# Outputs of six expert pairs of the last layer sent through DRAM rows by token, in place of one-hot products

## The chip, the core and the metric

The program runs on one core of a Trainium2 chip. Its five engines work side by side: TensorE (PE, matrix products), VectorE (DVE), ScalarE (ACT), GpSimd (POOL) and SyncE (SP), and all DMA traffic of the core goes over 16 DMA engines. The metric is the device time of one execution in microseconds (us), lower is better; several executions are timed and their median is given. A profiled execution leaves a trace with the start and the length of every instruction, and of every DMA packet.

## What is computed

A diffusion transformer of two layers, in float32: 256 tokens `x`, 256 context tokens `ctx`, width 1024, 16 experts of width 256. The second layer is the last one and does its expert part for the 256 tokens of `x` alone. Cut to what matters here:

```python
def moe_ffn(h, w_router, router_bias, w_gate, w_up, w_down):
    ...  # each token takes the two best experts of one group of four
    gates = jnp.sum(jax.nn.one_hot(expert_idx, N_EXPERTS, dtype=f32) * w[..., None], axis=1)
    out = jnp.zeros_like(t)
    for e in range(N_EXPERTS):
        hid = jax.nn.silu(t @ w_gate[e]) * (t @ w_up[e])
        out = out + gates[:, e:e + 1] * (hid @ w_down[e])
    return out.reshape(shape)

# in the layer:  x = x + g2 * moe_ffn(hx, ...);  after the last layer:  rms_norm(x, final_g)
```

## The kernel before

Each token has exactly two experts, so the kernel computes an expert for the tokens that chose it alone. In the last layer the function `expert_pairs` takes the experts two at a time, pairs 0 to 7, each expert with a list of 64 places, so that a pair fills 128 places. A ninth unit (number NP = 8) is a single expert that has more tokens than 64 places hold. Which token stands in which place is kept in one-hot matrices `route.sel[i]` (128 tokens of tile i by all places, T = 2 tiles).

The steps of pair p, in the code's names: `gather` brings the tokens of four experts into their places by one-hot products (L1134); `half(p, 0)` and `half(p, 1)` are the gate and the up products (L1169; L1156 for the single expert) into the one bank `gu`; `hidden` is SiLU on ACT (L1179) and a product on DVE (L1180), which frees `gu`; `turn` transposes the hidden layer (L1190) and the one-hot places (L185) on PE; `down` is the third product (L1217); `evacuate` multiplies by gate and modulation on DVE (L1202) and splits the result in two float32r parts, `yh` on ACT (L1204) and `yl` on DVE (L1205); `add` sums both parts into four accumulators by one-hot products (L1235). At the end `sum_` adds the accumulators to x, and the last norm and the stores follow.

The loop runs over p, and PE's order in a turn of it is half(p,0), turn(p-1), add(p-2), half(p,1), down(p-1), gather. DVE, ACT, POOL and SP each take their own instructions in order; a scheduler wrote that order when the program was built.

Weights are 1 MB each (six per pair), issued by SP into 13 slots in the order of their use: a load starts when a slot has been read for the last time. The three weights of the single expert are chosen at run time and are loaded by POOL with an indirect DMA (L353). POOL's DMAs run on queue q0, SP's on q1, ACT's on q10; the last norm's weights `fg` are loaded by ACT (L233).

Of the kernel before, what the change touches and what calls it, by code (L numbers as in the profile page):

```python
# [23 lines left out]
D = 1024  # L24
# [8 lines left out]
# columns of the packed constants  # L33
C_COS, C_SIN, C_MASK, C_IOTA, C_TRI, C_LT, C_GW, C_TOK, C_MH, C_EXP, C_ROW, C_SUM, C_END = (
    0, 128, 256, 512, 640, 768, 784, 788, 796, 804, 820, 821, 837)

# slots for raw weights: throughout, from the output projection on, from the experts on
RAW = dict(A=4, B=(4, 3), C=(2, 5))
# halves of units as float32r parts: projections, their outputs' projections, experts
WSP = dict(proj=4, out=(4, 4), moe=5)  # L40
# banks of PSUM in the phases of a layer
# [17 lines left out]
TICK = (("sums", 1), ("high", 5), ("transposes", 0), ("evacuate", 0), ("weights", 1), ("finish", 0), ("scores", 3),  # L59
        ("low", 5), ("maxima", 3), ("finish", 2), ("finish", 1), ("exps", 3), ("rest", -1), ("values", -1))  # L60
# halves of experts' weights that are ready ahead of their products
LEAD = 4
OVERFLOW = True
# products that keep the array's clock up before the experts
# [7 lines left out]
def shape_constants():  # L72
    """Constants that depend on shapes alone, packed [128, C_END]."""
# [21 lines left out]
    k[:, C_SUM:C_END] = i % 32 == np.arange(16)  # L95
# [3 lines left out]
class Ring:  # L99
    """Weights in the order of their use, loaded ahead into whatever slots are free."""  # L100
# [11 lines left out]
    def open(self, pool, tag, n, last, queue=None):  # L112
        """n slots, for units of layers up to last"""
        self.free.extend((pool, f"{tag}{i}" if n > 1 else tag, last) for i in range(n))
        self.load(queue)
# [52 lines left out]
class Model:  # L168
# [38 lines left out]
    def rstd(self, pool, ss, n, width, tag):  # L207
        """(ss / n + eps) ** -0.5 over [128, width]"""
# [12 lines left out]
    def split(self, raw, lo, hi, engine=None):  # L221
        """A half of a unit of raw weights as an exact sum of two float32r parts."""
# [7 lines left out]
    def bcast(self, pool, tag, src, n, name, bufs=1, queue=None):  # L230
        """n elements in DRAM over all partitions"""
# [6 lines left out]
    def run(self, over):  # L238
        tc, nc, a = self.tc, self.nc, self.a
        self.over = over  # L240
        with ExitStack() as ctx:
# [9 lines left out]
            self.yrows = self.dram.tile([NEXP * SLOTS * max(self.npass), D], F32, name="yrows")  # L251
            self.ada_in()
# [25 lines left out]
    def queue(self):  # L278
        """The weights in the order of their use."""
# [15 lines left out]
        def block(name, l, cb, n):  # L295
            for h in range(2):
# [3 lines left out]
                if name == "w_out" and h:  # L300
                    # rows of heads (kind, key head, query) to chunks of (kind, query)
# [6 lines left out]
        for l in range(2):  # L308
# [28 lines left out]
    def warm(self, n):  # L337
        """Products that nothing uses: the array's clock is to be up when the next ones come"""
# [87 lines left out]
    def ada_third(self, l, third):  # L426
        """2048 columns of the modulation: the four 512s land on partitions 32j (c) and 32j+1 (c_ctx)."""
# [42 lines left out]
        elif third == 1:  # L470
            # what the shift adds to the router's logits, over all partitions
# [25 lines left out]
    # steps and the loads of units in a third of the modulation  # L497
    STEPS = (9, 10, 9)

    def fill(self, n):  # L500
        """n steps of the modulation among other work"""
# [3 lines left out]
    # rows of the modulation in DRAM: (third, half)  # L505
# [8 lines left out]
    def layer(self, l):  # L514
# [28 lines left out]
        self.nt2 = 8  # L543
        with self.psums(PS_ATT):
            self.attention(l)
# [33 lines left out]

    def t2(self, name):  # L580
# [8 lines left out]
    def parameters(self, l):  # L589
        """The small parameters of a layer's attention"""  # L590
# [19 lines left out]
        def lam():  # L610
            """-(exp1 - exp2 + lam0)"""
# [6 lines left out]
    def tokens_in(self, l, tl):  # L618
        """Steps that bring tiles of a stream, normalized and modulated, to d on the partitions in Xh and Xl"""
# [22 lines left out]
        # the chunks of d in a bank  # L642
# [35 lines left out]
    def chunk(self, ps, tiles, kc, parts):  # L678
        """The products of tiles with a chunk of d of the first block of the projections"""
# [7 lines left out]
    def first_in(self):  # L687
        """The tokens of the first layer, half of d after the other, with the first block of its projections"""
# [99 lines left out]
            # the context's tokens have had their last use  # L788
# [3 lines left out]
    def parts(self, name, l, cb, fill=(0, 0)):  # L792
        """The halves of two units, split"""
# [9 lines left out]
    def units(self, name, l, cb, pairs, xh, xl, c0, parts):  # L803
        """The products of tiles of tokens with 512 columns of a weight, a group of tiles after another."""
# [15 lines left out]
    def rope(self, dst, src, nh, t, view=lambda z: z):  # L820
        """dst, src: [128, nh * 64]"""
# [17 lines left out]
    def head_norm(self, src, nh, g):  # L839
        """src: [128, nh * 64] in PSUM -> SBUF"""  # L840
# [33 lines left out]
    def project_in(self, l, first):  # L874
        nc, nq = self.nc, self.nq
        tile_ = lambda name, *shape, dt=F32: self.qkv.tile([128, *shape], dt, name=name)
        # by head and map
# [5 lines left out]
        for i, cb in enumerate(CBS):  # L883
# [3 lines left out]
            for t, ps in products:  # L887
# [46 lines left out]
    def attention(self, l):  # L934
        """All heads, as a pipeline of items: two maps of scores of a tile of queries each."""
# [28 lines left out]
    def out_proj(self, l, work, mods):  # L964
        """x += g1 (mix w_out), and the routing of the tiles as they get ready"""
# [20 lines left out]
    def experts(self, l, mo, lists):  # L986
        """One expert after another, the second half of its layers among the next one's first half"""
# [4 lines left out]
        # halves of weights in the order of their use, some of them ahead of it  # L992
# [28 lines left out]
        def tokens(n):  # L1021
            """What an expert gets, with d on the partitions"""
# [10 lines left out]
        def first(n, b, s):  # L1033
            """Half the products of the gate or of the up projection"""
# [15 lines left out]
        def turn(n):  # L1050
            # f = p * 2 + c
# [55 lines left out]
    def expert_pairs(self, l, mo, route):  # L1107
        """Two experts at a time on halves of the columns of the array; gathers and sums by one-hot products."""
# [804 lines left out]
```

## Time and profile before

| | us |
|---|---|
| median of 3 timed runs (lowest, highest) | 903.25 (901.96, 904.15) |
| span of the profiled execution, first to last instruction | 900.9 |
| PE busy in it | 799.3 (89%) |
| DVE busy | 584.3 |
| ACT busy | 453.6 |
| POOL busy | 211.5 |
| chain that ended last: share of PE | 70% |

The span is that of one profiled execution; the timed runs hold what lies around the span as well, 2.4 us here by the median. Busy shares are means over stages that are limited by different things, so the stage of the change is read by itself, in stretches of the span.

### The profile page before, as it was taken

The numbers are of one execution on the slowest core, as the hardware profiler recorded it, in microseconds if no ns is written. First come the engines' busy times: TensorE is split into PE (matmuls) and PEld (weight loads), VectorE is DVE, ScalarE is ACT, GpSimd is POOL, SyncE is SP. The second block draws the span as 40 slices with busy tenths as digits, with TensorE's granted clock in tenths as the row PEclk, the third lists the DMA queues.
The fourth block names the chain that finished last, engine by engine and source line by source line (L and its number), as shares of the span: only waits on it lengthen the run. The fifth ranks groups of instructions, "written<-read, shape, count | busy, mean of one in ns | idle before, by whom it ended". The sixth has DMA issues, their size and how long they took to land.

```text
span 900.9 us, 13085 instructions
## 1 busy us (share of the span) xinstructions
PE 799.3 (89%) x4807; PEld 584.2 (65%) x4807; DVE 584.3 (65%) x1192; ACT 453.6 (50%) x877; POOL 211.5 (23%) x244
## 2 busy tenths in 40 slices
PE   4899999989889977999999459999799869999992
PEld 1578877545546746999999348767566647666551
DVE  1577673897942698899999487677587563231224
ACT  2454432777652426888888456443387442121112
POOL 2010102473320133443432561000442000000100
PEclk9999999999998998999999769999999988999996
DMA  9952221666579537899993754287035965999921
GB/s 320 346 171 92 93 94 47 249 227 235 181 239 343 192 141 261 310 402 399 402 406 146 256 202 187 90 327 281 0 132 152 354 245 220 406 406 407 378 84 51
DMA packets 52537, 213.34 MB, mean 237 GB/s; under 512 B 9756, under 2 KB 9756, under 8 KB 34672
## 3 DMA queue, kind: packets, MB, share of 16 engines
q1 hardware_dynamic: 40832, 182.34, 54.4%
q0 software_dynamic: 6752, 19.08, 6.3%
q10 hardware_dynamic: 4880, 11.00, 3.2%
q8 instruction: 40, 0.66, 0.3%
q14 instruction: 33, 0.27, 0.1%
HBM read 204.99 MB, written 11.60 MB: 240 GB/s over the span
## 4 chain that ended last, share of the span: by engine, by line
PE 70%; DVE 14%; issue 4%; DMA 4%; ACT 4%; POOL 3%; ACTq 0%; SPq 0%; POOLq 0%; DVEq 0%
PE mm L199 8%; PE mm L197 8%; PE mm L198 8%; PE gu L1169 7%; PE tp L185 5%; PE gu L199 4%; PE w L1217 3%; PE gu L197 3%; PE gu L198 3%; PE ada L448 3%; DVE nm L1407 2%; PE w L1134 2%; PE sc L1393 2%; PE acc L1235 2%; PE y L197 2%
## 5 line engine op out<-in xcount | busy, mean ns | idle before, releaser
L227 DVE TENSOR_TENSOR wlo<-wraw,whi 128x1024 fp32r<-128x1024 f32 x136 | 186.5, 1391 | 51.9 <-ACT whi L226 51.1
L226 ACT CAST whi<-wraw 128x1024 fp32r<-128x1024 f32 x152 | 153.0, 1050 | 73.5 <-PE mm L199 39.1
L197 PE MATMUL mm<-whi,Xh 128*128 128x512 f32 x288 | 117.9, 409 | 5.1 <-ACT Xh L670 4.7
L198 PE MATMUL mm<-wlo,Xh 128*128 128x512 f32 x288 | 115.6, 401 | 0.4 <-DVE wlo L227 0.4
L199 PE MATMUL mm<-whi,Xl 128*128 128x512 f32 x288 | 115.3, 400 | 0.5 <-DVE Xl L674 0.5
L213 POOL TENSOR_TENSOR rstd<-ms,cst 128x1 f32<-128x1 f32 (+2 forms) x36 | 30.2, 838 | 315.0 <-DVE ms L211 306.1
L1420 ACT ACTIVATE e<-sc,nm 128x512 f32<-128x512 f32 (+1 forms) x96 | 58.3, 613 | 37.1 <-DVE nm L1413 19.2
L199 PE MATMUL gu<-whi,xl 128*128 128x256 f32 x256 | 73.9, 289 | 0.2 <-DVE xl L1030 0.2
L197 PE MATMUL gu<-whi,xh 128*128 128x256 f32 x256 | 73.7, 288 | 0.3 <-ACT xh L1029 0.3
L198 PE MATMUL gu<-wlo,xh 128*128 128x256 f32 x256 | 72.3, 282 | 0.0
L197 PEld LDWEIGHTS mm<-whi,Xh 128*128 128x128 f32 x288 | 54.9, 191 | 23.9 <-ACT Xh L670 6.2
L199 PEld LDWEIGHTS mm<-whi,Xl 128*128 128x128 f32 x288 | 54.9, 191 | 14.6 <-DVE Xl L674 1.5
L198 PEld LDWEIGHTS mm<-wlo,Xh 128*128 128x128 f32 x288 | 55.1, 191 | 13.1 <-DVE wlo L227 1.2
L1169 PE MATMUL gu<-wraw,xq 128*64 128x256 f32 x512 | 62.5, 388 | 0.0
L227 POOL TENSOR_TENSOR wlo<-wraw,whi 128x1024 fp32r<-128x1024 f32 x16 | 42.5, 2656 | 81.3 <-ACT whi L226 50.3
L199 PEld LDWEIGHTS gu<-whi,xl 128*128 128x128 f32 x256 | 48.9, 191 | 1.3 <-DVE xl L1030 0.6
L1169 PEld LDWEIGHTS gu<-wraw,xq 128*64 128x64 f32 x512 | 36.2, 138 | 20.8 <-issue 4.1
L197 PEld LDWEIGHTS gu<-whi,xh 128*128 128x128 f32 x256 | 49.1, 192 | 0.5 <-ACT xh L1029 0.5
L198 PEld LDWEIGHTS gu<-wlo,xh 128*128 128x128 f32 x256 | 49.0, 191 | 0.0
L185 PEld LDWEIGHTS tp<-ident,e 128*128 128x128 f32 x240 | 26.3, 143 | 34.7 <-issue 15.3
L1407 DVE TENSOR_REDUCE nm<-sc 128x1 f32<-128x512 f32 x64 | 41.6, 684 | 10.9 <-PE sc L1393 7.2
L1180 DVE TENSOR_TENSOR hid<-hid,gu 128x256 f32<-128x256 f32 (+1 forms) x9 | 3.8, 422 | 64.9 <-ACT hid L1179 64.9
(329 smaller groups left out, 1689.2 us busy)
## 6 DMA issues: line engine op xcount, KB each, us to landing
wraw<-in_w_ada SPq DMA_DIRECT2D x40, 1024.0 KB, 4.7
wraw<-in_w_gate SPq DMA_DIRECT2D x32, 1024.0 KB, 9.6
wraw<-in_w_up SPq DMA_DIRECT2D x32, 1024.0 KB, 9.9
wraw<-in_w_down SPq DMA_DIRECT2D x32, 1024.0 KB, 8.6
wraw<-in_w_in SPq DMA_DIRECT2D x16, 1024.0 KB, 6.9
wraw<-in_w_ada SPq DMA_DIRECT2D x16, 512.0 KB, 8.0
yrows<-y ACTq DMA_DIRECT2D x16, 512.0 KB, 7.4
wraw<-in_w_out SPq DMA_DIRECT2D x4, 1024.0 KB, 7.8
```

Of the source, the lines that this page charges most:

```text
L185: self.nc.tensor.transpose(out, in_, self.k["ident"][:n, :n])
L197: mm(out, lhsT=xh, rhs=wh, start=start, stop=False)
L198: mm(out, lhsT=xh, rhs=wl, start=False, stop=False)
L199: mm(out, lhsT=xl, rhs=wh, start=False, stop=stop)
L213: nc.gpsimd.tensor_tensor(r, ms, self.k["mhalf"][:, :width], OP.pow)
L226: nc.scalar.copy(h, raw[:, lo:hi])
L227: (engine or nc.vector).tensor_tensor(l, raw[:, lo:hi], h.bitcast(F32), OP.subtract)
L448: nc.tensor.matmul(ps[32 * j:32 * j + 32, :], lhsT=self.silu_c[:, kc, :], rhs=raw[:, 512 * j:512 * j + 512], start=kc == 0, stop=kc == NKC ...
L1169: nc.tensor.matmul(gu[PSLOTS * g:PSLOTS * g + PSLOTS, 256 * b:256 * b + 256], lhsT=xq[q][:, kc, c:c + PSLOTS], rhs=raw[:, kc * 256:kc * 25 ...
L1217: nc.tensor.matmul(y[hf][gs], lhsT=hT[:, c, 0:PSLOTS] if p == NP else hT[:, c, gs], rhs=raw[:, c * D + o * 512:c * D + o * 512 + 512], sta ...
L1407: V.reduce_max(self.nm[:, i:i + 1], self.ps[i], axis=AX.X)
L1420: nc.scalar.activation(self.e[i][:, :self.nkey], self.ps[i], AF.Exp, scale=0.125, bias=self.nm[:, i:i + 1], accum_out=self.z[i])
```

## The change

In the first six pairs (`SCATTER = 6`) the outputs are no longer split, turned and added by one-hot products. `evacuate` writes one float32 tile `yr`, and POOL scatters its 128 rows with an indirect DMA to a DRAM tensor `prow` of 512 rows: each token has two rows, one for each of its experts. Places without a token carry a row number outside the tensor and are not written. `rows_back` reads `prow` back into four tiles of 128 x 1024, and `add_back` adds them to x on DVE. Pairs 6 and 7 and the single expert keep the old way. `prow` is cleared in the last layer's attention by one 2 MB store. The row numbers come out of the product that gave the gates by place, which now multiplies the places with 48 columns (`picks`: two parts of the gate, and the row) in float32r, in place of 16 in float32.

```diff
+SCATTER = 6
+            self.prow = self.dram.tile([PROWS, D], F32, name="prow")
...
+    def clear_rows(self):
+        z = self.per.tile([128, 512], F32, tag="modrow", name="zeros")
+        self.nc.gpsimd.memset(z, 0.0)
+        rows = self.prow[:, :].rearrange("(p a) (b n) -> p (a b) n", a=4, n=512)
+        self.nc.sync.dma_start(rows, z.unsqueeze(1).broadcast_to([128, 8, 512]))
...
         def turn(p):
...
             nc.scalar.copy(hT[:, :, :n], w[:, 0:2 * P2].rearrange("p (c s) -> p c s", s=P2)[:, :, :n])
+            if p < SCATTER:
+                return
             w = self.bank("w")
...
         def evacuate(p, o, y, g):
+            if p < SCATTER:
+                nc.vector.scalar_tensor_tensor(st[p]["y"][0][:, o], y, gates[:, p:p + 1], g, OP.mult, OP.mult)
+                return
...
         def down(p):
...
+            if p < SCATTER:
+                nc.gpsimd.indirect_dma_start(
+                    out=self.prow[:, :], out_offset=bass.IndirectOffsetOnAxis(ap=rows[:, p:p + 1], axis=0),
+                    in_=st[p]["y"][0], in_offset=None, bounds_check=PROWS - 1, oob_is_err=False)
+
+        def rows_back():
+            src = self.prow[:, :].rearrange("(i p r) d -> i r p d", i=T, r=2)
+            back = [[self.pm.tile([128, D], F32, tag=f"{n}{i}", name="back") for n in ("hh", "hl")] for i in range(T)]
+            for i in range(T):
+                for r in range(2):
+                    nc.gpsimd.dma_start(back[i][r], src[i, r])
+            return back
+
+        def add_back(back, i, r):
+            x = self.x[self.qtiles[i]]
+            nc.vector.tensor_tensor(x, x, back[i][r], OP.add)
...
-        for p in range(len(pairs)):
+        for p in range(NP):
             for i in range(T):
-                nc.tensor.matmul(w[:, p * 16:p * 16 + 16], lhsT=route.sel[i][:, p * P2:p * P2 + P2].bitcast(F32),
-                                 rhs=(route.gf if p == NP else route.g)[:, i], start=i == 0, stop=i == T - 1)
+                nc.tensor.matmul(w[:, p * 48:p * 48 + 48], lhsT=route.sel[i][:, p * P2:p * P2 + P2],
+                                 rhs=route.picks[:, i].rearrange("p a e -> p (a e)"), start=i == 0, stop=i == T - 1)
...
-            if 0 <= p - 2 < NP - 1:
+            if SCATTER <= p - 2 < NP - 1:
                 add(p - 2)
...
-            elif p == 6:
+            elif p == SCATTER:
+                back = rows_back()
                 xq[4] = self.bcast(mo, "xq", self.a["final_g"], D, "fg", 2)
+            if p == NP:
+                for i in range(T):
+                    for r in range(2):
+                        add_back(back, i, r)
```

The scheduler decides where the new instructions stand on each engine. On DVE, the order before from pair 6's `hid` to pair 6's outputs is this (`hid` reads and frees the bank `gu`; the first two `u` with their `yl` are the evacuation of pair 5, `hid_8537` is that of pair 7, the last two `u` the evacuation of pair 6):

```order
L1180 TENSOR_TENSOR hid_8461<-hid_8461,gu_8398 128x256
L1202 SCALAR_TENSOR_TENSOR u_8476<-w_8466,pgates_7787,g2_7682 128x512
L1205 TENSOR_TENSOR yl_8465<-u_8476,yh_8464 128x512
L1202 SCALAR_TENSOR_TENSOR u_8480<-w_8467,pgates_7787,g2_7682 128x512
L1205 TENSOR_TENSOR yl_8465<-u_8480,yh_8464 128x512
L1180 TENSOR_TENSOR hid_8537<-hid_8537,gu_8486 128x256
L1202 SCALAR_TENSOR_TENSOR u_8552<-w_8542,pgates_7787,g2_7682 128x512
L1202 SCALAR_TENSOR_TENSOR u_8556<-w_8543,pgates_7787,g2_7682 128x512
```

With the change the same stretch of DVE reads as follows (`hid_8389` is that of pair 6, `yr` the evacuation of pair 5, L1267 is `add_back`, `hid_8461` is that of pair 7):

```order
L1195 TENSOR_TENSOR hid_8389<-hid_8389,gu_8339 128x256
L1219 SCALAR_TENSOR_TENSOR yr_8392<-w_8393,pgates_7800,g2_7687 128x512
L1219 SCALAR_TENSOR_TENSOR yr_8392<-w_8394,pgates_7800,g2_7687 128x512
L1267 TENSOR_TENSOR x2_107<-x2_107,back_8408 128x1024
L1267 TENSOR_TENSOR x2_107<-x2_107,back_8409 128x1024
L1267 TENSOR_TENSOR x3_108<-x3_108,back_8410 128x1024
L1267 TENSOR_TENSOR x3_108<-x3_108,back_8411 128x1024
L1195 TENSOR_TENSOR hid_8461<-hid_8461,gu_8418 128x256
L1222 SCALAR_TENSOR_TENSOR u_8476<-w_8466,pgates_7800,g2_7687 128x512
L1222 SCALAR_TENSOR_TENSOR u_8480<-w_8467,pgates_7800,g2_7687 128x512
```

The four additions of `add_back` stand right behind the evacuation of pair 5, and ahead of the `hid` of pair 7 and the evacuation of pair 6.

On POOL, the last layer's expert stage before holds three DMAs only, the weights of the single expert:

```order
L1115 COPY g2x_7684<-g2_7682 64x512 x2
L353 DMA wraw_8362<-in_w_gate,extra_7749 128x2048
L353 DMA wraw_8415<-in_w_up,extra_7749 128x2048
L353 DMA wraw_8457<-in_w_down,extra_7749 128x2048
L213 TENSOR_TENSOR rstd_8672<-ms_8670,cst_61 128x1
L213 TENSOR_TENSOR rstd_8679<-ms_8677,cst_61 128x1
```

With the change the six scatters and the four reads stand among them (`prow<-yr` is a scatter, the first shown that of pair 3; `back<-prow` is a read):

```order
L1252 DMA prow_100<-yr_8199,prows_7801 512x1024
L359 DMA wraw_8306<-in_w_gate,extra_7762 128x2048
L1252 DMA prow_100<-yr_8293,prows_7801 512x1024
L359 DMA wraw_8356<-in_w_up,extra_7762 128x2048
L359 DMA wraw_8385<-in_w_down,extra_7762 128x2048
L1252 DMA prow_100<-yr_8392,prows_7801 512x1024
L1262 DMA back_8408<-prow_100 128x1024
L1262 DMA back_8409<-prow_100 128x1024
L1262 DMA back_8410<-prow_100 128x1024
L1262 DMA back_8411<-prow_100 128x1024
```

The last scatter, that of pair 5, comes behind all three weights, and the four reads behind it; each scatter waits for the one before it to have landed, since all write the same tensor, and the reads wait for the last one.

## Rows read from the trace of the kernel before

**Rows 1.** Windows of the expert stage: stretch, length, busy times, granted clock, DMA share, GB/s.

```profile
775.00:835.00 60.00, 60.00 (x426) 37.49 (x422) 16.15 (x27) 12.57 (x27) 0.00 (x0) 1.00 1.00 410
835.00:846.00 11.00, 11.00 (x71) 6.30 (x68) 4.40 (x7) 2.81 (x6) 1.81 (x2) 1.00 0.92 325
846.00:861.00 15.00, 15.00 (x103) 8.93 (x103) 3.22 (x5) 2.85 (x7) 1.31 (x2) 1.00 0.96 403
```

**Rows 2.** Chain that ended last, one turn of the loop: start us, us, what.

```profile
793.66 3.60 PE gu L1169 x32
...
797.71 0.22 PE w L185 x2
797.92 1.85 PE acc L1235 x8
...
808.91 3.60 PE gu L1169 x32
```

**Rows 3.** The chain's gates by place, and a window of the clock behind them.

```profile
753.34 2.56 PE w L1249 x22
...
756.90:760.30 3.40, 3.40 (x14) 1.77 (x14) 0.50 (x3) 0.00 (x0) 0.00 (x0) 0.50 0.84 277
```

**Rows 4.** DVE in order of time: evacuation of pair 5, hid of pair 7, late additions.

```profile
855.38 0.74 DVE L1202 SCALAR_TENSOR_TENSOR u<-w,pgates,g 128x512 f32<-128x512 f32 x1
...
864.97 0.42 DVE L1180 TENSOR_TENSOR hid<-hid,gu 128x256 f32<-128x256 f32 x1 [7.47 <-ACT hid L1179]
...
887.21 1.28 DVE L1291 TENSOR_TENSOR x<-x,fg 128x512 f32<-128x512 f32 x2
```

**Rows 5.** DMA view: landings of POOL's DMAs (three windows), bytes from 757 to 861 us.

```profile
DMA packets 5619, 40.46 MB, mean 389 GB/s; under 512 B 622, under 2 KB 622, under 8 KB 750
...
xg<-h2row,idx POOLq DMA_INDIRECT x7, 9.5
...
yc<-yrows,rows POOLq DMA_INDIRECT x8, 5.9
...
g<-modrow POOLq DMA_DIRECT2D x1, 512.0 KB, 9.6
```

**Rows 6.** DMA view from 742 to 744 us: what each queue moved.

```profile
q1 hardware_dynamic: 73, 0.47, 63.0%
q0 software_dynamic: 66, 0.27, 35.2%
```

**Rows 7.** POOL in order of time: a DMA's landing waited for, an indirect issue.

```profile
746.88 1.28 POOL L1115 COPY g2x<-g 64x512 f32<-64x512 f32 x2 [9.07 <-DMA g<-modrow]
839.44 1.10 POOL L353 DMA_INDIRECT wraw<-in_w_gate,extra  x1 [91.28 <-PE w L1134]
```

**Rows 8.** SP's queue in order of time, and its wait view: waiter, waited for, us.

```profile
829.01 6.41 SPq L149 DMA_DIRECT2D wraw<-in_w_up  x2
843.78 8.08 SPq L149 DMA_DIRECT2D wraw<-in_w_down  x4
...
SPq L149 <- DMA fg<-in_final_g: 8.3, 1, 8.3
```

**Rows 9.** Chain that ended last: pair 7's up products, single expert's first, the last piece.

```profile
860.90 3.60 PE gu L1169 x32
...
865.79 0.10 PE gu L1156
...
890.45 0.72 ACT fo L1296
```

**Rows 10.** PE behind two waits: an instruction in order of time, and windows of the clock.

```profile
526.07 1.97 PE L185 MATMUL tp<-ident,xn 128*128 128x128 f32 x8 [20.44 <-DVE xn L635]
...
529.40:535.00 5.60, 5.06 (x11) 3.57 (x12) 4.90 (x7) 2.71 (x4) 4.57 (x5) 0.50 0.10 18
742.90:746.70 3.80, 3.73 (x18) 3.49 (x18) 1.69 (x10) 0.57 (x1) 0.00 (x0) 0.50 1.00 389
```

**Rows 11.** Window of the last layer's attention, where the rows are cleared.

```profile
629.00:658.00 29.00, 23.80 (x112) 17.21 (x114) 18.06 (x37) 13.34 (x34) 14.35 (x26) 0.94 0.01 2
```

More of the change, by code (lines that the diff above doesn't have):

```diff
@@ L31 @@
 PSLOTS = 64
-C_COS, C_SIN, C_MASK, C_IOTA, C_TRI, C_LT, C_GW, C_TOK, C_MH, C_EXP, C_ROW, C_SUM, C_END = (
-    0, 128, 256, 512, 640, 768, 784, 788, 796, 804, 820, 821, 837)
+PROWS = 512
+SCATTER = 6
+C_COS, C_SIN, C_MASK, C_IOTA, C_TRI, C_LT, C_GW, C_TOK, C_MH, C_EXP, C_ROW, C_SUM, C_PAIR, C_END = (
+    0, 128, 256, 512, 640, 768, 784, 788, 796, 804, 820, 821, 837, 839)
 RAW = dict(A=4, B=(4, 3), C=(2, 5))
@@ L94, in shape_constants @@
     k[:, C_ROW:C_SUM] = i
-    k[:, C_SUM:C_END] = i % 32 == np.arange(16)
+    k[:, C_SUM:C_PAIR] = i % 32 == np.arange(16)
+    k[:, C_PAIR:C_END] = 2 * (np.arange(2)[None, :] * 128 + i) - PROWS
     return k
@@ L543, in layer @@
         self.nt2 = 8
+        if self.paired(l):
+            self.clear_rows()
         with self.psums(PS_ATT):
@@ L1207, in down @@
         def down(p):
-            st[p]["y"] = [mo.tile([128, D], F32R, tag=t, name=t, bufs=2) for t in ("yh", "yl")]
+            if p < SCATTER:
+                st[p]["y"] = [mo.tile([128, D], F32, tag="yh", name="yr", bufs=2)]
+            else:
+                st[p]["y"] = [mo.tile([128, D], F32R, tag=t, name=t, bufs=2) for t in ("yh", "yl")]
             y, hT = [self.bank("w") for _ in range(1 if p == NP else 2)], st[p]["hT"]
@@ L1227, in down @@
                 evacuate(p, o, y[hf], g2[:, o])
+            if p < SCATTER:
+                nc.gpsimd.indirect_dma_start(
[11 more added lines that the diff above has]
+            nc.vector.tensor_tensor(x, x, back[i][r], OP.add)
         def add(p):
@@ L1235, in add @@
                         nc.tensor.matmul(acc[i][hf], lhsT=st[p]["sT"][s, i * 128:i * 128 + 128],
-                                         rhs=y[s, o:o + 512], start=p == h == 0, stop=p == NP and h == 1)
+                                         rhs=y[s, o:o + 512], start=p == SCATTER and h == 0, stop=p == NP and h == 1)
         gather(0, 0)
@@ L1246, in expert_pairs @@
         w = self.bank("w")
-        for p in range(len(pairs)):
+        for p in range(NP):
             for i in range(T):
-                nc.tensor.matmul(w[:, p * 16:p * 16 + 16], lhsT=route.sel[i][:, p * P2:p * P2 + P2].bitcast(F32),
-                                 rhs=(route.gf if p == NP else route.g)[:, i], start=i == 0, stop=i == T - 1)
-        gates = mo.tile([128, NP + 1], F32, name="pgates")
+                nc.tensor.matmul(w[:, p * 48:p * 48 + 48], lhsT=route.sel[i][:, p * P2:p * P2 + P2],
+                                 rhs=route.picks[:, i].rearrange("p a e -> p (a e)"), start=i == 0, stop=i == T - 1)
+        for i in range(T):
+            nc.tensor.matmul(w[:, 400:416], lhsT=route.sel[i][:, NP * P2:NP * P2 + P2].bitcast(F32),
+                             rhs=route.gf[:, i], start=i == 0, stop=i == T - 1)
+        gates, rows = mo.tile([128, NP + 1], F32, name="pgates"), mo.tile([128, NP], I32, name="prows")
         for g in range(2):
             gs = slice(PSLOTS * g, PSLOTS * g + PSLOTS)
-            nc.vector.tensor_copy(gates[gs, :NP], w[gs, 0:NP * 18].rearrange("p (a b) -> p a b", b=18)[:, :, g])
-        nc.vector.reduce_sum(gates[:, NP:], w[:, NP * 16:NP * 16 + 16], axis=AX.X)
+            v = w[gs, 0:NP * 50].rearrange("p (a b) -> p a b", b=50)
+            nc.vector.tensor_copy(gates[gs, :NP], v[:, :, g])
+            nc.vector.tensor_tensor(gates[gs, :NP], gates[gs, :NP], v[:, :, 16 + g], OP.add)
+            nc.vector.tensor_scalar(rows[gs], v[:, :, 32 + g], float(PROWS), None, OP.add)
+        nc.vector.reduce_sum(gates[:, NP:], w[:, 400:416], axis=AX.X)
         for p in range(len(pairs) + 1):
@@ L1270, in expert_pairs @@
                 gather(p // 2 + 1, p % 2)
-            elif p == 6:
+            elif p == SCATTER:
+                back = rows_back()
                 xq[4] = self.bcast(mo, "xq", self.a["final_g"], D, "fg", 2)
+            if p == NP:
+                for i in range(T):
+                    for r in range(2):
+                        add_back(back, i, r)
         add(NP - 1)
@@ L1599, in __init__ @@
             self.pe, self.g, self.gf = (m.pm.tile([128, T, 16], F32, name=n) for n in ("pe", "g", "gf"))
+            self.picks = m.pm.tile([128, T, 3, 16], F32R, name="picks")
             return
@@ L1684, in choose @@
         for n, z in enumerate((self.part[:, i * 128:i * 128 + 128], part)):
-            nc.tensor.matmul(lg, lhsT=z, rhs=cst[:, C_SUM:C_END], start=n == 0, stop=n == 1)
+            nc.tensor.matmul(lg, lhsT=z, rhs=cst[:, C_SUM:C_PAIR], start=n == 0, stop=n == 1)
         if self.paired:
@@ L1720, in choose @@
         V.scalar_tensor_tensor(cand, top, gm, cst[:, C_GW:C_GW + 4], OP.is_equal, OP.mult)
+        if self.paired:
+            rank = self.gf[:, i].rearrange("p (g e) -> p g e", e=4)
         V.reduce_sum(rank, gt, axis=AX.X)
@@ L1813, in places, with pick @@
         V.tensor_scalar(g, g, gsum, None, OP.mult)
+        self.late.append(lambda: self.pick(i))
+    def pick(self, i):
+        V, g, z = self.nc.vector, self.g[:, i], self.picks[:, i]
+        self.nc.gpsimd.tensor_copy(z[:, 0], g)
+        V.tensor_tensor(z[:, 1], g, z[:, 0].bitcast(F32), OP.subtract)
+        z2 = self.gf[:, i]
+        V.tensor_scalar(z2, z2, self.k["cst"][:, C_PAIR + i:C_PAIR + i + 1], None, OP.add)
+        V.scalar_tensor_tensor(z[:, 2], self.pe[:, i], 0.0, z2, OP.is_gt, OP.mult)
     def count(self):
@@ L1824, in extra @@
         small = lambda n, name: self.small([n], name)
-        f, nf, mx, fe, eid = small(16, "f"), small(1, "nf"), small(1, "mx"), small(16, "fe"), small(1, "eid")
+        f, nf, mx, fe, eid = small(16, "f"), small(1, "nf"), small(1, "mx"), small(16, "pf"), small(1, "eid")
         V.tensor_scalar(f, cnt, float(PSLOTS), None, OP.is_gt)
```

## The prediction

> **What bounds the kernel now.** I read the windows first, then the chain, then the DMA view, and last the queues' own orders. In the expert stage the windows show two things that are full at once: PE is busy in all of every stretch at full clock, and the DMA engines are busy 1.00 of 775 to 835 us at 410 GB/s [rows 1]. The chain says which of them ends the work: a turn of the loop is 808.91 - 793.66 = 15.25 us of PE pieces without a gap [rows 2], so weights are always there in time, and PE sets the pace. But the DMA is close behind. A turn takes six loads of 1.05 MB, 6.29 MB, which at 410 GB/s are 15.3 us. What keeps weights out of the chain is their lead: the ups of pair 7 are issued from 829.0 us on and used at 860.9 [rows 8, 9]. Whatever makes PE faster here eats that lead, and whatever adds bytes eats it from the other side. The change does both.
>
> **What is removed on PE.** The adds of pairs 0 to 5 cost 1.85 us each and the transposes of their places 0.22 us [rows 2]: 6 x 2.07 = 12.4 us, all on the chain. The gates by place are 36 instructions at 2.56 / 22 = 0.116 us [rows 3], 4.2 us. With the change they are 16 products of 48 columns and 4 old ones. The trace has no float32r product of 48 columns; bounds are the row's 0.116 us and twice that, so 2.3 to 4.2 us for the 20, and PE then also waits for a few more small DVE instructions, up to 1 us. Behind the gates stand 3.4 us at half clock [rows 3], which cost 1.7 us and may or may not come again. The gain is between 0 and 2.6 us; I take 1.8. On DVE and ACT the splitting of six pairs goes away, which is not on the chain. Hidden at no cost: the clearing store of 2 MB, since from 629 to 658 us the DMA moves 2 GB/s [rows 11], at 410 GB/s it needs 5 us, and those 29 us are idle on the queue; without that cover it would cost up to 5 us. Picking the row numbers adds some ten small instructions ahead of the gates, counted above.
>
> **What is added to the DMA.** Every token has two experts, so 512 rows of 4 KB in all; pairs 0 to 5 hold 12 of 16 experts, about 384 rows, 1.57 MB (at most all 512, 2.10 MB). The reads bring back 4 x 0.52 = 2.10 MB. Together 3.67 MB, at 410 GB/s 9.0 us more of an engine set that is already full: from 757 to 861 us it moved 40.46 MB at a mean of 389 [rows 5]. Against that stand two recoveries. The dip to 325 GB/s in 835 to 846 us [rows 1] is SP standing 8.3 us behind the landing of `fg` [rows 8]. With the change the load that waits for it is an earlier one, pair 7's ups, at a time when the queue has a backlog; I count the dip as regained, (410 - 325) x 11 / 410 = 2.3 us (the other bound is nothing). And the stage starts 1.8 us earlier. So the last byte lands at 861 + 9.0 - 2.3 - 1.8 = 866 us. What lands last are the reads, as follows.
>
> **When the reads come.** Pair 5's evacuation ends at 855.38 + 0.74 = 856.1 us [rows 4]. Ahead of it lie five adds and six transposes of places, 9.25 + 1.3 = 10.6 us, and 1.8 us of the gates, so it ends at 843.8 us. POOL then issues the scatter (1.10 us for an indirect DMA [rows 7]). No indirect store stands in the trace; the nearest rows are indirect reads on the same queue, 9.5 us to landing beside a full weight queue, 5.9 us without one [rows 5]. Here the queue is full: 9.5, so the scatter lands at 853.3 us and the reads start then. A read of their kind and size took 9.6 us [rows 5], with DVE-side waiting 9.07 us for it [rows 7], beside the same weights. Four of them are 2.10 MB. Beside a full weight queue POOL's queue got 0.27 of 0.74 MB in two microseconds [rows 6], 36%, or 150 GB/s: 14 us, that is 867 us, and a little less once the weights have ended. The two counts agree on 866 us.
>
> **What waits for them.** All four additions stand on DVE behind pair 5's evacuation and ahead of `hid` of pair 7, as the order shows. DVE cannot pass them. `hid` of pair 7 frees the only bank `gu`, so PE cannot begin the single expert, nor what stands behind it: the rest of pair 6's outputs, the adds of pairs 6 to 8 and the end. An addition of 128 x 1024 is bounded by two of 128 x 512, 1.28 us [rows 4]; three of the four hide behind the later reads' landings. So `hid` of pair 7 ends at 866 + 1.3 + 0.4 = 867.7 us, where before it ended at 864.97 + 0.42 = 865.4 [rows 4]: 2.3 us later, although PE has done pair 7's products at about 864.5 - 14.2 = 850 us (a few us later if its weights come late) and stands still for more than 10 us.
>
> From `hid` of pair 7 to the end both programs do the same: before, PE starts the single expert at 865.79 and the span ends at 900.9 [rows 9]. One thing differs, the clock. Behind a wait of 20.4 us PE worked at 0.50 for the 5.6 us from 529.4 to 535.0; behind shorter waits it worked 3.8 us at 0.50 from 742.9 to 746.7 [rows 10] before the granted clock was at its full level again. Half of that is lost: 1.9 to 2.8 us, and I take 2.3. In return PE, which before was still 0.4 us at pair 6's products when `hid` ended, can begin some 0.1 us behind it: 0.3 us.
>
> **Sum.** 900.9 + 2.3 + 2.3 - 0.3 = 905.2 us of span, 4.3 us above the profiled one. The median of the timed runs stands 2.4 us above that span: 903.25 + 4.3 = 907.5 us. The gain of 14.2 us on PE turns into a wait on DVE.
>
> **Rivals.** Faster: the reads land before the weights' backlog ends. For it speak the 5.9 us of indirect reads without weights beside them [rows 5]; with 5.9 for the scatter and for the last read, issued 1.8 us behind the first, they are in at 843.8 + 5.9 + 1.8 + 5.9 = 857.4 us, `hid` ends at 859.1, 6.3 us earlier than before, and with the clock's 2.3 us and the 0.3 the median is 898.9. Against it speaks that the weights then still come, and that rows 6 give POOL's queue little over a third. It decides from a landing at 861.7 us on: earlier is faster, later is slower.
>
> On this rival bears a rule of the Trainium skill, "DMA: Bandwidth & Descriptors", section "Anatomy of one DMA — SWDGE (gpsimd) path": it fits a transfer issued by GpSimd as 2.0 us plus its bytes at 436 GB/s, whatever else is moving. By it (an estimate) a read of 0.52 MB takes 3.2 us, all reads would be in near 854 us, and the time would be near 896. By that rule the trace does not agree: the same size took 9.6 us beside the weights [rows 5].
>
> No change: the reads land at 861 to 863 us, because DMA runs nearer 420 GB/s or fewer rows are written; 903 us. For it speaks how near the break-even lies.
>
> Much slower: stores to scattered rows are dearer than reads, all 512 rows are written, nothing of the dip is regained, nothing of the gates. 4.2 MB at 389 GB/s are 10.8 us: landing at 872, 914 us. Nothing in the trace prices such a store.
>
> **How the numbers follow.** Forecast 0.47, faster by early reads 0.25, no change 0.18, much slower 0.10. About 0.2% (1.8 us) is what a measurement of this kernel can tell from no change. So faster 0.25, same 0.18, slower 0.57. The range goes from below the early reads, 898 us, to near the dear stores, 913; the forecast's own is 904.5 to 911.
>
> **What would show it.** Right: DVE idle from about 844 us to beyond 862, released by the DMA `back<-prow`; PE idle ahead of the single expert's products for 10 us or more, and half clock behind it; adds of six pairs gone and 15.25 us a turn down to 13.2 up to pair 5; DMA full to 864 or later. Wrong: if `hid` of pair 7 is released by ACT and not by the reads, the early reads hold; if PE waits for weights in pairs 5 to 7 for many us, the bytes are dearer than I count; if the turns stay at 15 us, PE was not what bound them.

## The result and the profile after

The changed kernel takes 910.28 us (median of 8 runs, 906.91 to 912.65) against 904.53 us of the kernel before on the same chips (8 runs, 901.96 to 906.64): 1.0069 times as long, 95% interval 1.0053 to 1.0085, or 5 to 8 us. The forecast was 4.3 us more than before.

The profiled execution, the slowest of the eight, has a span of 910.8 us, 9.9 more than that of before, but nearly half of this lies ahead of the expert stage. POOL in order of time, first of the kernel before, then of the changed one, shows the same instructions right ahead of the stage:

```profile
736.59 0.68 POOL L213 TENSOR_TENSOR rstd<-ms,cst 128x1 f32<-128x1 f32 x1 [7.70 <-DVE ms L211]
737.21 0.59 POOL L233 DMA_DIRECT2D g<-modrow  x1
```

```profile
741.11 0.67 POOL L218 TENSOR_TENSOR rstd<-ms,cst 128x1 f32<-128x1 f32 x1 [7.70 <-DVE ms L216]
741.74 0.19 POOL L1874 CAST picks<-g 128x16 fp32r<-128x16 f32 x1
742.10 0.59 POOL L238 DMA_DIRECT2D g<-modrow  x1 [0.17 <-issue]
...
848.46 1.00 POOL L1252 DMA_INDIRECT prow<-yr,prows  x1 [6.04 <-DVE yr L1219]
858.12 2.16 POOL L1262 DMA_DIRECT2D back<-prow  x4 [8.66 <-DMA prow<-yr,prows]
```

`rstd` is 4.5 us later, and PE and DVE lie as far behind there; the load of `g` is 4.9 us later, because the cast of the new `picks` now stands ahead of it. Followed back through DVE's instructions, the two programs are 3.8 us apart already at 600 us, ahead of everything that the change touches there, above all by steps near 160 and 340 us where PE was granted half clock for longer; the mean granted clock of the two executions is 0.952 and 0.937. At the same place the traces of the eleven experiments below, which all hold parts of the change, lie between 0.5 us ahead of before and 3.9 us behind it. So this is the spread from one execution to the next, and 4.5 us are taken off every time of the changed kernel below before it is set against one of before.

Windows of the expert stage (columns as in [rows 1]):

```profile
775.00:835.00 60.00, 60.00 (x434) 36.15 (x432) 14.90 (x24) 9.27 (x19) 6.04 (x6) 1.00 1.01 414
835.00:846.00 11.00, 10.48 (x76) 5.54 (x73) 0.70 (x2) 1.13 (x3) 2.03 (x2) 1.00 1.01 418
846.00:861.00 15.00, 11.57 (x68) 6.47 (x66) 1.22 (x2) 0.00 (x0) 3.16 (x5) 0.77 1.02 421
861.00:872.00 11.00, 2.02 (x8) 0.57 (x6) 5.14 (x5) 0.38 (x1) 0.00 (x0) 0.79 0.63 254
```

The dip to 325 GB/s of [rows 1] is gone: the DMA moves 414 to 421 GB/s without a gap to 861 us. In the last two windows PE is busy 13.6 of 26 us; before it was busy all of 846 to 861 us. PE in order of time says what it stands for:

```profile
757.01 2.13 PE L1289 MATMUL w<-picks,sel 128*128 128x48 f32 x16
...
759.65 0.40 PE L1292 MATMUL w<-gf,sel 128*128 128x16 f32 x2
...
766.16 3.67 PE L1184 MATMUL gu<-wraw,xq 128*64 128x256 f32 x32
...
792.53 3.67 PE L1184 MATMUL gu<-wraw,xq 128*64 128x256 f32 x32
...
842.36 0.51 PE L1205 MATMUL w<-ident,hid 128*128 128x128 f32 x2
843.38 0.44 PE L190 MATMUL w<-ident,sel 128*128 128x128 f32 x2 [0.52 <-ACT hT L1207]
843.75 2.36 PE L1240 MATMUL w<-wraw,hT 128*64 128x512 f32 x9
...
854.92 6.23 PE L1184 MATMUL gu<-wraw,xq 128*64 128x256 f32 x29 [3.41 <-DMA wraw<-in_w_up]
...
871.63 2.40 PE L1171 MATMUL gu<-wraw,xq 128*64 128x256 f32 x9 [8.97 <-DVE hid L1195]
```

Two turns are 792.53 - 766.16 = 26.37 us, one 13.2, against 15.25 before [rows 2]. The third product of pair 5 (L1240) now has the transposes of pair 6 within it, to 843.75 us; in the chain of before it ran in one piece:

```profile
851.52 3.43 PE w L1217 x16
```

Then come two waits that before did not have: 3.4 us for pair 7's ups, and 9.0 us for `hid` of pair 7 on DVE. DVE in order of time, of the changed kernel and (one line) of the kernel before:

```profile
847.43 0.75 DVE L1219 SCALAR_TENSOR_TENSOR yr<-w,pgates,g 128x512 f32<-128x512 f32 x1 [0.96 <-PE w L1240]
866.37 4.88 DVE L1267 TENSOR_TENSOR x<-x,back 128x1024 f32<-128x1024 f32 x4 [18.18 <-DMA back<-prow]
871.16 0.41 DVE L1195 TENSOR_TENSOR hid<-hid,gu 128x256 f32<-128x256 f32 x1
877.06 0.75 DVE L1222 SCALAR_TENSOR_TENSOR u<-w,pgates,g 128x512 f32<-128x512 f32 x1 [5.48 <-PE w L1240]
```

```profile
868.46 0.75 DVE L1202 SCALAR_TENSOR_TENSOR u<-w,pgates,g 128x512 f32<-128x512 f32 x1 [3.07 <-PE w L1217]
```

DVE stands 18.2 us for the rows read back. ACT had finished the SiLU of pair 7 at 861.8 us; `hid`, which needs nothing else, starts 9.4 us later because the four additions are ahead of it. Behind the two waits PE runs at half clock (windows):

```profile
853.75:860.58 6.83, 5.66 (x28) 3.20 (x30) 0.00 (x0) 0.00 (x0) 2.16 (x4) 0.50 1.02 421
867.40:877.64 10.24, 6.01 (x19) 2.40 (x20) 4.69 (x6) 0.00 (x0) 0.00 (x0) 0.50 0.09 34
```

With 4.5 us off, the kernel is behind the one before by 1.7 us when `hid` of pair 7 starts ([rows 4]: 864.97), 4.1 us at the evacuation of pair 6 (877.06 against 868.46), 4.5 us at the last piece of ACT (899.43 against 890.45, [rows 9]), and 5.4 us at the end of the span.

The DMA view's landings, of the scatters and the reads:

```profile
back<-prow POOLq DMA_DIRECT2D x4, 512.0 KB, 9.1
...
prow<-yr,prows POOLq DMA_INDIRECT x6, 8.9
```

### The profile page after: what moved, and what is told of

It is laid out like the page before. It is cut to its first block, busy times and chain, and to the rows that moved or that the text cites. A ratio compares the mean times of both kernels' runs of the same rounds, so it can differ in the third digit from the quotient of the medians.

```text
span 910.8 us, 12948 instructions
## 1 busy us (share of the span) xinstructions
PE 797.2 (88%) x4731; PEld 579.4 (64%) x4731; DVE 582.5 (64%) x1194; ACT 445.8 (49%) x859; POOL 221.5 (24%) x257
## 3 DMA queue, kind: packets, MB, share of 16 engines
q0 software_dynamic: 8192, 22.82, 7.2%
## 5 line engine op out<-in xcount | busy, mean ns | idle before, releaser
L1184 PE MATMUL gu<-wraw,xq 128*64 128x256 f32 x512 | 64.7, 396 | 3.4 <-DMA wraw<-in_w_up 3.4
L203 PEld LDWEIGHTS mm<-wlo,Xh 128*128 128x128 f32 x288 | 55.2, 192 | 13.1 <-DVE wlo L232 1.2
L232 POOL TENSOR_TENSOR wlo<-wraw,whi 128x1024 fp32r<-128x1024 f32 x16 | 42.4, 2655 | 81.3 <-ACT whi L231 50.3
L190 PEld LDWEIGHTS tp<-ident,e 128*128 128x128 f32 x240 | 26.9, 145 | 36.0 <-issue 16.4
L190 PE MATMUL tp<-ident,e 128*128 128x128 f32 x240 | 38.7, 291 | 7.5 <-DVE e L1512 3.8
```

The costliest lines, as they stand in the source:

```text
L190: self.nc.tensor.transpose(out, in_, self.k["ident"][:n, :n])
L203: mm(out, lhsT=xh, rhs=wl, start=False, stop=False)
L232: (engine or nc.vector).tensor_tensor(l, raw[:, lo:hi], h.bitcast(F32), OP.subtract)
L1184: nc.tensor.matmul(gu[PSLOTS * g:PSLOTS * g + PSLOTS, 256 * b:256 * b + 256], lhsT=xq[q][:, kc, c:c + PSLOTS], rhs=raw[:, kc * 256:kc * 25 ...
```

## The experiments

The theory: DVE's order holds the end, since the additions stand ahead of `hid` of pair 7 and their data are the last bytes of a DMA that is full. The rivals: the bytes alone (late weights) hold it; or the reads are late because they are asked late, behind the scatter's landing.

### The additions behind the single expert's hid

```diff
-            nc.vector.tensor_tensor(hid[d], hid[d], gu[d, 256:512], OP.mult)
+            st[p]["prod"] = nc.vector.tensor_tensor(hid[d], hid[d], gu[d, 256:512], OP.mult)
...
                 hidden(p)
+                if p == NP:
+                    with self.tc.issue_after(st[p]["prod"].ins):
+                        for i in range(T):
+                            for r in range(2):
+                                add_back(back, i, r)
...
-            if p == NP:
-                for i in range(T):
-                    for r in range(2):
-                        add_back(back, i, r)
```

> The four additions of the rows read back stand on DVE behind the single expert's hid instead of ahead of pair 7's; nothing else is moved. Theory A (the prediction's: DVE's order holds the end): hid of pair 7 starts as soon as ACT has done SiLU, at about 861.8 us of the changed kernel's profile instead of 871.2, PE has no wait of 9.0 us ahead of the single expert and no half clock behind it (2.8 us); 910.3 - 9.4 - 2.8 + 1 for additions that have to wait for the last read = 899 us. Rival B (the added bytes hold the end: pair 7's weights come late and the order on DVE is no matter): PE waits for weights in place of DVE, under 3 us gained, 907 us or more.

Measured: 897.19 us, 0.992 of before (0.9902 to 0.9939); 13.1 us less than the changed kernel. DVE and then PE in order of time:

```profile
857.04 0.42 DVE L1195 TENSOR_TENSOR hid<-hid,gu 128x256 f32<-128x256 f32 x1 [13.75 <-ACT hid L1194]
...
865.53 4.63 DVE L1267 TENSOR_TENSOR x<-x,back 128x1024 f32<-128x1024 f32 x4
```

```profile
850.33 6.04 PE L1184 MATMUL gu<-wraw,xq 128*64 128x256 f32 x29 [3.11 <-DMA wraw<-in_w_up]
```

`hid` is now released by ACT, and the additions find their rows there. Theory A holds: with every byte still moved, the place of four instructions on one engine is worth 13 us and the sign of the change. What is left is the wait for pair 7's ups.

### Reads that do not wait for the scatter

```diff
+            self.pclear = self.dram.tile([PROWS, D], F32, name="pclear")
...
-        rows = self.prow[:, :].rearrange("(p a) (b n) -> p (a b) n", a=4, n=512)
+        rows = self.pclear[:, :].rearrange("(p a) (b n) -> p (a b) n", a=4, n=512)
...
-            src = self.prow[:, :].rearrange("(i p r) d -> i r p d", i=T, r=2)
+            src = self.pclear[:, :].rearrange("(i p r) d -> i r p d", i=T, r=2)
...
-                back = rows_back()
+                with self.tc.issue_after(last[0].ins):
+                    back = rows_back()
```

> The four reads take a second tensor that nothing is scattered to (the sums leave the first six pairs out), behind the last scatter on POOL's queue but without the wait of 8.7 us for its landing; additions in the changed kernel's place. Theory A (the reads are late because they are asked late): they are issued at 849.5 instead of 858.1 us, land by about 861, hid of pair 7 is released by ACT at about 862, 910.3 - 9 - 2.8 = 899 us. Rival B (the DMA engines are full, so reads asked earlier only share with the weights): they get half of 420 GB/s and need 10 us or more, pair 7's ups come up to 5 us later, hid of pair 7 ends at 865 to 868, 903 to 906 us.

Measured: 910.03 us, 1.006 (1.0039 to 1.0081): nothing gained, less than even rival B gave. The reads were issued at 849.1 us, 9 us sooner. DVE's additions:

```profile
860.87 1.22 DVE L1268 TENSOR_TENSOR x<-x,back 128x1024 f32<-128x1024 f32 x1 [13.02 <-DMA back<-pclear]
864.76 1.23 DVE L1268 TENSOR_TENSOR x<-x,back 128x1024 f32<-128x1024 f32 x1 [2.67 <-DMA back<-pclear]
867.79 1.22 DVE L1268 TENSOR_TENSOR x<-x,back 128x1024 f32<-128x1024 f32 x1 [1.80 <-DMA back<-pclear]
869.79 1.22 DVE L1268 TENSOR_TENSOR x<-x,back 128x1024 f32<-128x1024 f32 x1 [0.78 <-DMA back<-pclear]
```

The first rows come 5.5 us sooner, the last at the same time (869.79; in the changed kernel the fourth addition starts at about 870.0). So here neither waiting for the scatter's landing nor being asked 9 us later sets the end of the reads; what is the same in both kernels is the bytes that the two queues have to move by then. The DMA view of this kernel from 856 to 864 us, and that of the changed kernel from 844 to 852 us, where POOL's queue carries the single expert's weights, show how the queues share (packets, MB, share of the DMA):

```profile
q1 hardware_dynamic: 300, 2.18, 65.8%
q0 software_dynamic: 315, 1.12, 34.9%
```

```profile
q1 hardware_dynamic: 233, 1.71, 51.5%
q0 software_dynamic: 224, 1.68, 50.3%
```

Both times the two queues moved about as many packets as each other, 315 to 300 and 224 to 233. The reads' packets are 4 KB and get a third of the bytes; the indirect loads' are 8 KB, as large as those of SP's weights, and get half. On this the Trainium skill, "DMA: Bandwidth & Descriptors", section "Queues, rings and completion order", says that each DMA engine goes round the queues that have work, a packet at a time, with some 9 to 17 descriptors in a packet. The trace agrees as far as both queues moved about as many packets as it counts; it does not show where a packet of that rule ends.

### Five pairs in place of six, without and with the additions moved

```diff
-SCATTER = 6
+SCATTER = 5
...
-            elif p == SCATTER:
+            if p == SCATTER:
                 back = rows_back()
+            if p == 6:
                 xq[4] = self.bcast(mo, "xq", self.a["final_g"], D, "fg", 2)
```

> Five pairs scattered in place of six; the reads are then asked one turn sooner, and pair 5 is added by products again. Theory A (asked late): reads are issued near 843 us, land near 855, the additions are done before hid of pair 7 is wanted; PE pays 2.1 us for one more add: 910.3 - 12.2 + 2.1 = 900 us, up to 903 if the reads push weights back. Rival B (bytes): the 2.1 MB now lie ahead of pairs 6 and 7's weights, PE waits 5 to 8 us for them, 905 us or more.

Measured: 917.2 us, 1.0144 (1.012 to 1.0168). Neither number was right; the block had only moved. The scheduler now put three of the additions ahead of the `hid` of pair 6 (PE, then DVE):

```profile
857.81 0.70 PE L1205 MATMUL w<-ident,hid 128*128 128x128 f32 x2 [20.07 <-DVE hid L1195]
```

```profile
848.72 1.22 DVE L1267 TENSOR_TENSOR x<-x,back 128x1024 f32<-128x1024 f32 x1 [19.89 <-DMA back<-prow]
...
857.34 0.41 DVE L1195 TENSOR_TENSOR hid<-hid,gu 128x256 f32<-128x256 f32 x1
859.97 1.23 DVE L1267 TENSOR_TENSOR x<-x,back 128x1024 f32<-128x1024 f32 x1 [2.21 <-DMA back<-prow]
```

The same with the additions where the first experiment has them:

> As e3 (five pairs, reads asked one turn sooner) but the additions stand behind the single expert's hid, as in e1. Theory A (e3's 917 us is the block on DVE and nothing else; PE sets the pace): e1 and one more add with its transposes, 897.2 + 2.1 = 899.3 us. Rival B (the DMA sets the end of the stage): pair 7's ups land when they do in e1, PE's wait for them shrinks by what PE loses, 897 us. Rival C (reads in front of the weights cost as much as the block): 905 us or more.

Measured: 904.82 us, 1.0014 (0.9998 to 1.0031). 12.4 us of the 917.2 were the block, but what is left is 5.5 us above the 899.3 of theory A, and near rival C. POOL, then PE:

```profile
843.72 2.17 POOL L1262 DMA_DIRECT2D back<-prow  x4 [11.97 <-issue]
846.20 1.05 POOL L359 DMA_INDIRECT wraw<-in_w_up,extra  x1 [0.30 <-issue]
```

```profile
865.33 1.97 PE L1171 MATMUL gu<-wraw,xq 128*64 128x256 f32 x8 [7.53 <-DMA wraw<-in_w_up,extra]
```

The reads now stand ahead of the single expert's up weights in POOL's own queue, and PE waits 7.5 us for these. POOL issues them only at 846.2 us (in the first experiment the same load was issued at 832.7, in a trace 3.1 us ahead of this one at 600 us), because it stands 12.0 us ahead of the reads, which wait for the landing of the last scatter. How much of the wait is this late issue, and how much the reads' bytes, these runs do not separate. Reads that are asked early are paid for by whatever comes behind them.

### What lies in front of pair 7's ups

In the next two kernels the norm's weights and the single expert's down weights change their place (both hold the first experiment's edit).

```diff
-                xq[4] = self.bcast(mo, "xq", self.a["final_g"], D, "fg", 2)
+                xq[4] = self.bcast(mo, "xq", self.a["final_g"], D, "fg", 2, queue=self.nc.gpsimd)
```

> As e1, and the last norm's weights are loaded by POOL behind the four reads instead of by ACT, so that SP's queue does not stand 11.6 us behind their landing ahead of pair 7's ups. Theory A (the standing queue makes the ups late): PE's wait of 3.4 us for these ups and 3.4 us at half clock (1.7 to 3.4 us lost) go away: 4 to 5 us below e1, 895 us. Rival B (the DMA engines are full at 1.00 from 823 to 861 us, so a queue that stands costs nothing): ups land as before, e1 plus or minus 1 us.

Measured: 898.41 us, 0.9928 (0.9907 to 0.995), as rival B has it, but the kernel was not what the text says: POOL issued the load at 828.42 us, ahead of all it was to follow, and PE's wait for the ups was 3.9 us. SP no longer stood: it issued these ups at 824.2 and 827.8 us, 6 and 3 us before those of the first experiment, in a trace that is 4.1 us behind that one at 600 us, and they came no sooner. It shows only that SP's standing queue (11.6 us behind `fg` in the changed kernel) is not what makes the ups late.

```diff
+                if name == "w_down":
+                    ring.add((name, l, 0, e), lambda t: setattr(self, "xdown", lambda: extra(name, t, n)))
+                    return
...
                 back = rows_back()
+                with self.tc.issue_after(last[0].ins):
+                    self.xdown()
```

> As e1, and the load of the single expert's down weights (1 MB, POOL's queue) is issued behind the four reads instead of 836.5 us, ahead of the last scatter. In e1 POOL's queue takes half of 420 GB/s from 838 to 848 us, just when pair 7's ups are on their way, and PE waits 3.1 and 0.6 us for these and works 6.8 us at half clock. Theory A (bytes in front of the ups set their landing): 1.05 MB less ahead of them, ups 2.5 us sooner, and up to 1.7 us of the half clock back: 893 to 895 us. Rival B (the ups' place in SP's own queue sets it): e1 plus or minus 1 us. Rival C: the moved load is now late for the single expert's products, and PE waits there instead: 897 us or more.

Measured: 893.58 us, 0.9873 (0.985 to 0.9896): theory A. PE's wait is down and the half clock behind it gone:

```profile
852.29 3.45 PE L1187 MATMUL gu<-wraw,xq 128*64 128x256 f32 x29 [1.61 <-DMA wraw<-in_w_up]
```

Then the norm's weights really behind it, in one block with the down load:

```diff
-                xq[4] = self.bcast(mo, "xq", self.a["final_g"], D, "fg", 2)
...
                     self.xdown()
+                    xq[4] = self.bcast(mo, "xq", self.a["final_g"], D, "fg", 2, queue=nc.gpsimd)
```

> As e5, and the last norm's weights (0.52 MB) are issued by POOL behind the single expert's down load, which e4 meant to do: there POOL issued them at 828.4 us, ahead of everything. Theory A (bytes in front of pair 7's ups set their landing): 0.52 MB less, 1.3 us sooner, PE's wait of 1.6 us goes to about 0.3: 892.4 us. Rival B (that wait has another cause): e5 plus or minus 0.5 us, and PE's wait stays at 1.6 us.

```profile
846.75 3.45 PE L1187 MATMUL gu<-wraw,xq 128*64 128x256 f32 x29 [0.28 <-DMA wraw<-in_w_up]
```

Measured: 891.23 us, 0.9861 (0.9843 to 0.9879). The wait is 0.28 us, as theory A said; this is the fastest full version, 13.5 us below the kernel before. Same bytes, same work, another order. By the ratios to before, the step from the last kernel is 1.1 us and within both intervals; for the cause of the wait the trace speaks, not the time.

### The parts alone

```diff
-SCATTER = 6
+SCATTER = 0
...
-            elif p == SCATTER:
-                back = rows_back()
+            if p == 6:
                 xq[4] = self.bcast(mo, "xq", self.a["final_g"], D, "fg", 2)
...
-                        add_back(back, i, r)
```

> Nothing scattered or read back, all pairs added by products as in the kernel before; what stays of the change are the gates by products of 48 columns and the clearing of the rows. Theory A (the prediction): 1.8 us gained, the clearing hidden, 902.7 us; by the profile after, which has the gates 3.6 us shorter, 900.9 us. Rival B (PE has 3.6 us more lead over nothing: weights come when they come): 904.5 us, no change. Rival C (the clearing costs): up to 5 us more than these.

Measured: 901.74 us, 0.9977 (0.9962 to 0.9993), 2 us below before (0.6 to 3.4 by the interval), nearer to the 1.8 us of the prediction than to 3.6. In its trace PE's distance to the kernel before falls from 4.1 to 0.9 us across the gates, by 3.2 us, and ends near there (a span of 901.5 us against 900.9). The kernel before has one trace, so whether it runs at half clock behind its gates each time, and where the other 1.1 us went, stays open. The clearing costs nothing that shows: in the changed kernel's trace PE's distance to before is 3.8 us at 590 us and, past the store, 3.4 to 3.8 us up to 648 us.

And the changed kernel without the rows, so that its sums lack the outputs of six pairs:

```diff
-            if p < SCATTER:
-                nc.gpsimd.indirect_dma_start(
...
-                back = rows_back()
...
-                        add_back(back, i, r)
```

> As the changed kernel without scatters, reads and additions (the outputs of six pairs are left out of the sums): PE's gain with none of the added bytes. Theory A (the added bytes still cost in e1, through pair 7's ups): no wait for these and no half clock, PE's 12.4 and the gates' 3.6 us come out in full, 904.3 - 16 = 888 to 890 us. Rival B (with PE faster, the weights' own bytes set the pace, and the added ones lie in gaps): 895 to 897 us, as e1.

Measured: 889.05 us, 0.9837 (0.9817 to 0.9857), theory A. So the rows cost 21 us as the change moves them, 8 us with the additions late, and 2 us in the best order. About 1 us of each of the three is the end of the program, which comes next.

### The end of the program

Two POOL instructions in the last 10 us of the program grew with the change; the traces call them DRAIN and INC_SWDGE_SEM. Their lengths in the traces, in this order:

| kernel | DMAs issued by POOL | their packets | the two, us |
|---|---|---|---|
| small loads on ACT | 62 | 7856 | 5.13 + 1.44 |
| before, gates alone, no rows | 66 | 6752 | 5.46 + 1.52 |
| changed kernel | 76 | 8192 | 6.28 + 1.72 |
| norm weights behind | 77 | 8336 | 6.36 + 1.74 |
| twenty small DMAs | 86 | 7392 | 7.09 + 1.92 |

> As e7, and POOL issues 20 more DMAs of one row of 64 B each behind the clearing in the last layer's attention, where it idles. The program's end holds two POOL instructions that are 1.0 us longer together in every run with ten more POOL DMAs than before (5.46 and 1.52 us with 66, 6.28 and 1.72 us with 76). Theory A (each DMA that POOL issued costs 0.10 us there): 7.1 and 1.9 us, 2.0 us over e7, 903.7 us. Rival B (the packets of these DMAs count, 144 each so far): with one row each they hold few, 0.3 us at most, 902 us.

```diff
+        for i in range(20):
+            c = slice(16 * i, 16 * i + 16)
+            self.nc.gpsimd.dma_start(y[0:1, c], self.a["final_g"].unsqueeze(0)[:, c])
```

The two instructions are 2.0 us longer, as theory A has it, while the packets grew by 640, less than half of the 1440 that came with 1.0 us in the changed kernel: it is the number of DMAs. The time, 914.0 us (1.0121, 1.0091 to 1.015), is no measure of that. POOL did not idle there: it waited 7.8 us for the clearing and issued for 9.5 us, and PE stood 8.3 us for the queries behind it.

```profile
639.44 9.54 POOL L597 DMA_DIRECT2D tiny<-in_final_g  x20 [7.82 <-DMA prow<-zeros]
```

> As e9, and 18 small loads of the modulation (biases and norm weights) are issued by ACT instead of POOL. Theory A (0.10 us for each POOL DMA at the end): the two last POOL instructions fall from 8.0 and more to 6.3 us, 1.8 us less than e9. Rival B (ACT stands behind what these loads wait for): PE waits for ACT in the first layers, as slow as e9 or slower.

```diff
-            dma(brow[r::32, :], src)
+            nc.scalar.dma_start(brow[r::32, :], src)
```

(and the same for the two norm weights). 15 DMAs executed fewer on POOL; the two instructions take 6.6 us in place of 8.1. The time is 892.27 us, 0.9862 (0.9842 to 0.9882): no gain over the 891.23 us. In the trace 1.3 us are lost in the last layer's attention, but one profile does not tell this from the spread of the runs, so where the 1.5 us went stays open.

## Why the prediction was right, point by point

- **PE's gain.** A turn of 13.2 us came as worked out. The gates gave more than the 1.8 us taken: 3.2 to 3.3 us in the traces. The products gave some 1.6, and the half clock behind the gates [rows 3], which was left out of the gain, did not come again in any of the twelve kernels with the new gates: another 1.7. The upper bound of 2.6 us was added up too low: 1.9 for the products and 1.7 for the clock are 3.6 when PE waits for nothing more.
- **The scatter's landing.** Pair 5's evacuation ended at 847.43 + 0.75 = 848.2 us, 843.7 with 4.5 off, against 843.8 in the prediction. That is partly luck: the gates gave 1.5 us more, and PE's order, taken as unchanged, lost about as much by subtraction, since the transposes of pair 6 now stand within the third product of pair 5 (L1205 and L190 at 842.36 and 843.38 us) and PE waits there for ACT. The landing was worked out as 9.5 us behind the issue; the read behind it was issued 9.7 us after it.
- **The DMA.** The dip was regained. By the trace's records the four reads landed at 866.3, 867.4, 868.7 and 869.9 us, and each addition follows its own, so three of them hide behind the later landings as worked out. The last landing is, with 4.5 us off, 0.6 us ahead of the 866 us of the sum. The share of POOL's queue, 36% by [rows 6], was 34.9% beside full weights (the reads that do not wait for the scatter). The reads took 9.1 us in the median, near the 9.6 of [rows 5]; the 9.07 us set beside this are a wait of POOL, and not on DVE's side [rows 7]. By the fit in the Trainium skill, "DMA: Bandwidth & Descriptors", section "Anatomy of one DMA — SWDGE (gpsimd) path", which has no term for other traffic, each would have taken 3.2 us (an estimate); the trace does not agree, here as before.
- **The block on DVE.** This was the step on which the sign hung, and the late additions show it: 13.1 us.
- **`hid` of pair 7.** 1.7 us later than before in place of 2.3, from the landing. PE stood 9.0 us for it, a little less than the 10 us named as the sign, because its own ups had come late.
- **The clock.** Worked out as 2.3 us, less 0.3: 2.0; measured from `hid` to pair 6's evacuation, 4.1 - 1.7 = 2.4 us.
- **What the sum left out.** 0.9 us at the end of the program, for ten more DMAs on POOL. And pair 7's ups came late, 3.4 us of waiting and half clock, named as possible ("a few us later if its weights come late"); it cost nothing here, since PE would have stood for `hid` anyway. It was the next limit as soon as the block was gone.
- **The rivals.** Early reads did not come: in the changed kernel's place, reads asked 9 us sooner still end at the same time. Asked a whole turn sooner, with five pairs, they did end ahead of the break-even of 861.7 us (the last addition starts at 859.97, in a trace 0.4 us ahead of before at 600 us), but there they stood in front of others and the kernel was slower still. So early landing is possible and its price lies elsewhere; a chance of 0.25 for the gain was too much.

Of the 5.4 us in the profile, 1.7 are the landing, 2.4 the clock, 0.4 between there and the last piece, 0.9 the end.

## What to carry to other kernels

An instruction that waits for a DMA costs what stands behind it on its engine, so look where the scheduler put it, and put it behind the last instruction that others wait for. Where the DMA is full, asking sooner gained nothing here or moved the wait to another transfer: order transfers by when their data are needed, across all queues, and first move back the ones that nobody needs yet. Count the DMAs that POOL issues: each is paid for once more at the end of the program.

## What was not expected of the hardware

Each DMA issued by POOL made two POOL instructions at the end of the program 0.10 us longer together (6.57 us with 62 of them, 9.01 with 86), whatever its size. Two full queues moved about equal numbers of packets, and so not of bytes: 4 KB packets against 8 KB got 34.9% of the DMA, 8 KB against 8 KB 50.3%. And two executions of programs that do the same up to there were 3.8 us apart at 600 us, the one with more half clock behind.
